# Loading the experts' weights in 2 MB parts through a ring of six buffers

## The chip, the core and the metric

The kernel runs on one core of one Trainium2 chip. The metric is the time of one execution on the device in microseconds; the median of several runs counts. All arithmetic on the path that matters here is in float32.

## What is computed

The reference is a model of two blocks over 512 tokens of width 1024. The first block and the first half of the second are mixers (attention, recurrences, projections). The change lies in the last stage, a mixture of experts: each token goes to 4 of 32 experts, each with a weight `w1` of 1024 x 2048 and a weight `w2` of 1024 x 1024. Cut to that:

```python
logits = ht @ router_w + router_b
top_val, top_idx = lax.top_k(logits, TOP_K)          # 4 of 32
gates = jax.nn.softmax(top_val, axis=-1)
...
def expert_block(args):
    idx, e = args
    u = clamped_swiglu(h_pad[idx] @ w1[e] + b1[e])
    return u @ w2[e] + b2[e]
...
y = jnp.zeros((t + 1, d)).at[slot_tok].add(y_slots * slot_gate[:, None])
```

After it a residual sum and a layer norm give the output of 512 x 1024.

## The kernel before

Engines are named as in the profile: PE is TensorE, PEld its weight loads, DVE VectorE, ACT ScalarE, POOL GpSimd, SP SyncE, whose queue issues most DMAs.

**The experts' stage** (`experts`, from L2173 on) goes through the 32 experts in an order that is worked out on the chip: place 0 is expert 0, the others are ordered by how many tokens they have. Each place has a fixed number of blocks of 32 rows (`BLOCKS`): one place has 4, sixteen have 3, fifteen have 2, mixed as the list `PLACES` (L35) says; 82 blocks in all. The index of an expert is read into a register of SP (L2200 and after), and its loads are addressed by it.

For place j the program issues `up` of j (L2300 on; first matrix product, 8 parts of the weight `w1`), then `down` of the place before it (L2360 on; second product, 4 parts of `w2`), so that the activation of j runs on DVE and ACT beside `down` of j - 1. Only place 0 is done alone: `up`, transposes, `down`. Inside `up` at fixed parts stand the other PE jobs: finding the rows of later experts (`slots`, at part 0), the transposes of the activations of the place before (`turn_u`, at part 2), and the transposes of the next place's rows (`turned`, at part 4), after which the gather for the place after that is issued on POOL. `down` ends with one scaling on DVE and one accumulating scatter on POOL for each block (L2380, L2381).

**A part** is 1 MB: 128 partitions of 2,048 float32, 8,192 bytes. An expert has 8 parts of `w1` (one for each 128 rows of the input) and 4 of `w2` (two 128-row pieces side by side), 12 MB; 32 experts make 384 parts. A block of a part takes 8 matmuls of 512 columns in `up` and 16 of 256 columns in `down`, as the profile counts them.

**The ring.** `ring` (L1829) sets the size of a part and makes a pool with 12 buffers, `EARLY`, on its first call, and a pool with one more on its second, when the experts' stage begins and space has come free; `RING` is 13. `load` (L1838) takes the buffers in turn: load n goes to buffer n modulo 13, and its DMA, issued on SP (L1843), waits until PE's last read of that buffer. So when a part has been used, the load that stands 13 later can be issued. The loads stand in SP's queue in the order in which PE uses them. In the tile framework the DMAs of SP use eight completion semaphores in turn, so that a load also waits for the landing of the DMA eight before it.

**The first twelve loads** are issued by `mix_out` (L1860), before the experts' stage, as `self.pre`: 8 parts of `up` and 4 of `down` of expert 0. They run beside the end of the mixer: the normalised rows are stored to `hd` in four stores of 512 KB from POOL (L1940), and the gather of the first expert's rows (L2274) reads `hd`. In `experts` a further line (L2184) would load what is missing of the first twelve; with `EARLY` 12 its range is empty. `up` and `down` take a part from `self.pre` while there are any, and call `load` afterwards.

**The end.** After the last `down` a check for experts with more rows than their places hold is made; for these inputs its branch is not taken. `final` (L2421 on) reads the scattered sums into the first four ring buffers, adds, normalises and stores the output.

Of the kernel before, what the change touches and what calls it, by code (L numbers as in the profile page):

```python
# [17 lines left out]
P = 128  # L18
# [3 lines left out]
D = 1024  # L22
KD = D // P
# [4 lines left out]
E = 32  # L28
TOPK = 4
LIMIT = 7.0  # L30
RING = 13
EARLY = 12


PLACES = [0, 17, 18]  # L35
# [1764 lines left out]
class Tail:  # L1800
# [20 lines left out]
    def weight(self, e):  # L1821

        w1, w2 = (self.k.I[n] for n in ("exp_w1", "exp_w2"))
        if isinstance(e, int):
            return (lambda i: w1[e, i * P:(i + 1) * P]), (lambda i: w2[e, i])
        return ((lambda i: w1[bass.ds(e, 1), i * P:(i + 1) * P].rearrange("a p n -> p (a n)")),
                (lambda i: w2[bass.ds(e, 1), i].rearrange("a p h n -> p (a h) n")))

    def ring(self, ctx):  # L1829

        k = self.k
        k.usize = 2 * D
        if not hasattr(self, "rings"):
            self.rings = [k.pool("rawx", 1, None, ctx, "left")] * EARLY
        else:
            self.rings += [k.pool("rawy", 1, None, ctx, "left")] * (RING - EARLY)

    def load(self, part):  # L1838

        self.loads += 1  # L1840
        n = self.loads % RING
        w = self.k.t(self.rings[n], [P, self.k.usize], tag=f"raw{n}", bufs=1)
        self.k.nc.sync.dma_start(w if len(part.shape) == 2 else w.rearrange("p (h n) -> p h n", h=2), part)  # L1843
        return w

    def mix_out(self, b):

        k = self.k
        nc, tc = k.nc, k.tc
        x3 = self.x3 = [k.t(b.mixp, [P, D], tag=f"ar{t}") for t in range(NT)]  # L1850
        self.yd = b.yd
        with ExitStack() as st:
            pw = k.pool("mow", 2, None, st)
            self.psp = b.psp
            for t in range(NT):
                nc.sync.dma_start(x3[t], b.base[t * P:(t + 1) * P])

            one, two = self.weight(0)
            self.loads = -1
            self.pre = [self.load(part) for part in ([one(i) for i in range(KD)] + [two(i) for i in range(4)])[:EARLY]]  # L1860
            self.first = k.t(b.po, [P, P], tag="po")

            def finish(t, nh, ps, r):
                ns = slice(nh * S, (nh + 1) * S)
                x = x3[t][:, ns]
                if nh == 0:
                    r.stats = k.t(pw, [P, 2, 6], tag="bn")
                    r.xT = k.t(pw, [P, KD, P], tag="xT")
                nc.vector.tensor_add(x, x, ps)
                pt = k.t(b.pa, [P, S], tag="pa")  # L1870
                for j in range(4):
                    nc.tensor.transpose(pt[:, j * P:(j + 1) * P], x[:, j * P:(j + 1) * P], k.ident)
                nc.scalar.copy(r.xT[:, nh * 4:nh * 4 + 4], pt.rearrange("p (a n) -> p a n", a=4))
                nc.vector.bn_stats(r.stats[:, nh], x)
                if nh:
                    self.norm(t, r, pw)


            n = 2 * NT
            rs = [SimpleNamespace() for _ in range(NT)]  # L1880
            routes = []
            done = []
            for i in range(n + 4):
                if i < 2:
                    done.append(b.made[i])
                elif i < n:
                    ps = k.t(b.pb, [P, S], tag="pb")
                    done.append((ps, b.product(*divmod(i, 2), ps)))
                with tc.issue_after(done[-1][1]):
                    if 1 <= i <= n:  # L1890
                        t, nh = divmod(i - 1, 2)
                        finish(t, nh, done[i - 1][0], rs[t])
                        if nh:
                            routes.append(self.route(t, rs[t], pw))
                    if i >= n:
                        routes.reverse()
                    routes = [g for g in routes if next(g, routes) is not routes]
            self.after = self.slots(pw, [0], self.first)
# [276 lines left out]
    def experts(self, ctx):  # L2175
        k = self.k
        nc, I, tc = k.nc, k.I, k.tc
        self.prev = None
        self.mw = mw = k.pool("moew", 2, None, ctx, "right")
        xg = [k.t(mw, [P, D], tag="xg") for _ in range(2)]  # L2180
        for x in xg:
            nc.vector.memset(x, 0.0)
        xg = self.gather(self.idx[:, 0:1])
        self.pre += [self.load(self.weight(0)[1](i)) for i in range(EARLY - KD, 4)]  # L2184
        self.biases(ctx)
        x = self.turned(xg)
        self.places_of(self.late)
        self.slots(mw, [1])
        xg = self.gather(self.idx[:, 1:2])

        self.gt2 = k.t(self.late, [P, 256], tag="gt2q")
        for n in range(4):
            v = MR["gt2"]
            nc.gpsimd.dma_start(self.gt2[n * 32:(n + 1) * 32], k.modr[v:v + 1, n * 256:(n + 1) * 256].to_broadcast([32, 256]))
        before = None
        for j in range(E):
            if j == 0:
                e, takes = 0, k.ident[:, 0:1]
            else:
                e = nc.values_load(self.order[0:1, j:j + 1], engines=[mybir.EngineType.SP], min_val=0, max_val=E - 1)  # L2200
                takes = self.takes[:, j:j + 1]
            nxt = SimpleNamespace(nb=BLOCKS[j], rows=self.rows[:, j], gate=self.gate[:, j])
            one, nxt.two = self.weight(e)
            then = {}
            if j % 2 == 0 and j + 2 < E:
                then[0] = lambda: self.slots(mw, [j + 2, j + 3])
            if before is not None and before.uT is None:
                then[2] = lambda: self.turn_u(before)
            if j + 1 < E:
                def following():  # L2210
                    nonlocal x, xg
                    x = self.turned(xg)
                    if j + 2 < E:
                        xg = self.gather(self.idx[:, j + 2:j + 3])
                if j:
                    then[4] = following
            self.up(nxt, x, takes, one, then)
            if before is not None:
                self.down(before)
            if j == 0:  # L2220
                self.turn_u(nxt)
                self.down(nxt)
                following()
                nxt = None
            before = nxt
            with tc.issue_after(self.sc):
                if j in (2, 10):
                    self.last_rows(j // 8)
                if j == E - 1:
                    self.final_rows()  # L2230
            if j in LB:
                with tc.issue_after(self.sc):
                    self.last_bias(*divmod(LB.index(j), NT))
        self.turn_u(before)
        self.down(before)

        self.rest(self.late)
        most = nc.values_load(self.over[0:1, E:E + 1], min_val=0, max_val=S)
        with tc.If(most > 0):
            self.make_lists(mw)  # L2240
            with tc.For_i(0, E, 1) as e:
                n = nc.values_load(self.over[0:1, bass.ds(e, 1)], min_val=0, max_val=S)
                with tc.If(n > 0):
                    self.more(e, 0)
                    for blk in range(1, NT):
                        with tc.If(n > P * blk):
                            self.more(e, blk)
# [49 lines left out]
    def up(self, st, x, takes, units, then):  # L2297


        k = self.k  # L2300
# [4 lines left out]
        with ExitStack() as order:  # L2305
# [3 lines left out]
            for i in range(KD):  # L2309
                if i in then:  # L2310
                    then[i]()
                w = self.pre.pop(0) if self.pre else self.load(units(i))
                for b in range(st.nb):
                    for c in range(4):
                        last = mm(ps[b][c * 32:(c + 1) * 32], x[:, i, b * 32:(b + 1) * 32], w[:, c * S:(c + 1) * S],  # L2315
# [43 lines left out]
    def down(self, st):  # L2359

        k = self.k
# [3 lines left out]
        of = lambda b: ps[b // 2][:, b % 2 * 256:(b % 2 + 1) * 256]  # L2365
        with tc.issue_after(self.prev):
            for c in range(4):
                w = (self.pre.pop(0) if self.pre else self.load(st.two(c))).rearrange("p (h n) -> p h n", h=2)
                for h in range(2):
                    for b in range(st.nb):  # L2370
                        for n in range(4):
# [107 lines left out]
def host(inp):  # L2479

    f = lambda a: np.ascontiguousarray(np.asarray(a))
# [8 lines left out]
    g = lambda n: np.asarray(inp[n])[0]  # L2490
# [19 lines left out]
    for n, a in (("ml_g", g("ml_norm_g")), ("gla_g", g("gla_norm_g")), ("final_g", inp["final_g"]),  # L2510
# [14 lines left out]
           "w_in_2": f(g("w_in_2")), "ada_w": f(g("ada_w_2")), "rwkv_w2": f(g("rwkv_w2_2")), "rwkv_a2": f(g("rwkv_a2_2")),  # L2525
           "rwkv_g2": f(g("rwkv_g2_2")), "w_uq": f(wuq), "w_kv": np.stack([g("w_uk_2"), g("w_uv_2")]),
           "pos": f(np.asarray(inp["positions_2"])[0].reshape(NT, P).T), "w_o": f(g("w_o_2")),
           "router_w": f(g("router_w_2")), "exp_w1": f(g("exp_w1_2")), "exp_w2": f(g("exp_w2_2").reshape(E, 4, 2, P, D).transpose(0, 1, 3, 2, 4)), "b1": f(g("exp_b1_2")),
           "b2": f(g("exp_b2_2"))}
    out.update(constants())  # L2530
    return out
# [15 lines left out]
```

## Time and profile before

| what | value |
|---|---|
| median of 3 runs | 1888.42 us (1884.67 to 1901.79) |
| the profiled execution, its own time | 1900.38 us |
| its span, first to last instruction | 1898.6 us |
| mean granted TensorE clock | 0.966 |
| PE busy | 1796.5 us, 95% of the span |
| experts' loads | 384 of 1,024 KB |

The profile shows one execution. The slices divide the span in forty, about 47.5 us each, and give the busy share in tenths; DMA is the mean busy share of the core's 16 DMA engines. A wait names the instruction that waited, what released it, the sum of the waiting times, how often, and the longest. PE's busy time counts pipelined matmuls, so 99% need not mean that it worked at its peak.

### The profile page before, as it was taken

What the parts mean: (1) busy time and instruction counts of PE and PEld (TensorE: products, weight loads), DVE (VectorE), ACT (ScalarE), POOL (GpSimd) and SP (SyncE); (2) the same over time, 40 slices, a digit from 0 to 9 for tenths busy, and PEclk for the clock granted to TensorE, in tenths of its full rate; (3) what the DMA queues carried; (4) which work ended last, traced back from release to release, by engine and by line L of the source; (5) the groups of instructions that cost most, each with busy time, mean ns of one, the idle gap of its engine ahead of it and who ended that gap; (6) DMA issues with size and microseconds to landing.
All of it is one profiled execution on the core that took longest, in us unless ns stands there. A gap on an engine that the chain in (4) does not pass through costs nothing. (4 is left out here: it accounts for less than half of the span.)

```text
span 1898.6 us, 40110 instructions
## 1 busy us (share of the span) xinstructions
PE 1796.5 (95%) x16798; PEld 1105.9 (58%) x16799; DVE 832.3 (44%) x2057; ACT 472.5 (25%) x1050; POOL 313.4 (17%) x285
## 2 busy tenths in 40 slices
PE   8999999998899999979999999999999999999982
PEld 8887788786798977744343434443444444344431
DVE  6756744756865577633233323232323222232323
ACT  4434323453345533311111111111111111111101
POOL 1010001032100014111113221123120212021102
PEclk9998979999899999989999999999999999999996
DMA  8255441655210013669999999999999999999994
GB/s 278 83 192 178 126 125 40 200 166 159 49 43 19 23 56 112 250 251 354 409 412 397 406 403 415 400 412 404 412 403 410 396 413 400 405 404 408 408 398 150
DMA packets 145212, 520.69 MB, mean 274 GB/s; under 512 B 29392, under 2 KB 71936, under 8 KB 95712
## 3 DMA queue, kind: packets, MB, share of 16 engines
q1 hardware_dynamic: 121360, 487.91, 65.8%
q0 software_dynamic: 18000, 22.06, 4.8%
q10 hardware_dynamic: 5664, 8.09, 1.4%
q8 instruction: 133, 2.18, 0.5%
q14 instruction: 55, 0.45, 0.1%
HBM read 504.30 MB, written 24.43 MB: 278 GB/s over the span
## 5 line engine op out<-in xcount | busy, mean ns | idle before, releaser
L2315 PE MATMUL h<-raw,x 128*32 128x512 f32 x5248 | 620.4, 596 | 4.5 <-DMA raw<-in_exp_w 4.4
L2315 PEld LDWEIGHTS h<-raw,x 128*32 128x32 f32 x5248 | 171.0, 110 | 346.8 <-issue 313.6
L2372 PE MATMUL y<-raw,uT 128*32 128x256 f32 x5248 | 293.2, 381 | 7.3 <-DMA raw<-in_exp_w 4.4
L2372 PEld LDWEIGHTS y<-raw,uT 128*32 128x32 f32 x5248 | 180.3, 110 | 126.8 <-issue 20.9
L2381 POOL DMA_INDIRECT yd<-y,rows x82 | 131.2, 1601 | 727.1 <-DVE y L2380 711.8
L2333 DVE TENSOR_TENSOR h<-h,bias 128x512 f32<-128x512 f32 x82 | 56.3, 687 | 309.9 <-PE h L2315 309.9
L2291 DVE TENSOR_SCALAR x<-ps,modc 128x128 f32<-128x128 f32 x128 | 52.0, 410 | 181.9 <-ACT x L2294 178.5
L2380 DVE SCALAR_TENSOR_TENSOR y<-y,gate,gt2q 128x256 f32<-128x256 f32 x82 | 35.2, 479 | 174.5 <-PE y L2372 174.5
L2341 ACT ACTIVATE sth<-sg 128x256 f32<-128x256 f32 x82 | 34.2, 417 | 266.5 <-DVE sg L2339 266.5
L155 PE MATMUL mm<-hh,hi 128*128 128x512 f32 (+1 forms) x248 | 97.7, 394 | 0.0
L156 PE MATMUL mm<-lo,hh 128*128 128x384 f32 (+4 forms) x288 | 95.4, 331 | 2.0 <-DVE lo L150 2.0
L156 PE MATMUL mm<-hl,hi 128*128 128x512 f32 (+1 forms) x248 | 96.4, 389 | 0.0
L155 PE MATMUL mm<-hi,hh 128*128 128x384 f32 (+4 forms) x288 | 95.8, 334 | 0.0
L157 PE MATMUL mm<-hh,lo 128*128 128x512 f32 (+1 forms) x248 | 95.0, 383 | 0.0
L157 PE MATMUL mm<-hi,hl 128*128 128x384 f32 (+4 forms) x288 | 94.4, 330 | 0.0
L150 DVE TENSOR_TENSOR lo<-raw,hi 128x1024 fp32r<-128x1024 f32 (+5 forms) x77 | 76.5, 997 | 40.0 <-ACT hi L149 38.9
L149 ACT CAST hi<-raw 128x1024 fp32r<-128x1024 f32 (+5 forms) x77 | 66.4, 863 | 101.8 <-PE mm L156 47.6
L2294 ACT ACTIVATE x<-ps,modc 128x128 f32<-128x128 f32 x128 | 57.1, 457 | 122.8 <-PE ps L2287 112.2
L2357 ACT COPY uT<-ps 128x512 f32<-128x512 f32 (+1 forms) x49 | 24.2, 518 | 161.4 <-PE ps L2354 157.9
L966 DVE SCALAR_TENSOR_TENSOR acc<-mraw,cact,acc 128x1024 f32<-128x1024 f32 x42 | 53.8, 1280 | 20.6 <-DMA mraw<-in_ada_w 20.4
L155 PEld LDWEIGHTS mm<-hi,hh 128*128 128x128 f32 x288 | 57.4, 199 | 7.3 <-issue 5.1
L2322 ACT COPY bias<-ps 128x512 f32<-128x512 f32 x32 | 18.8, 586 | 169.1 <-PE ps L2320 169.1
(720 smaller groups left out, 2730.4 us busy)
## 6 DMA issues: line engine op xcount, KB each, us to landing
raw<-in_exp_w SPq DMA_DIRECT2D x384, 1024.0 KB
mraw<-in_ada_w SPq DMA_DIRECT2D x48, 512.0 KB
raw<-in_w_in SPq DMA_DIRECT2D x30, 512.0 KB
raw<-in_w_in SPq DMA_DIRECT2D x16, 384.0 KB
raw<-in_w_out SPq DMA_DIRECT2D x8, 512.0 KB
raw<-in_w_o SPq DMA_DIRECT2D x16, 256.0 KB
yd<-x SPq DMA_DIRECT2D x5, 512.0 KB
x<-in_x SPq DMA_DIRECT2D x4, 512.0 KB
```

The source lines that it names most:

```text
L149: nc.scalar.copy(hi, r)
L150: nc.vector.tensor_sub(lo, r, hi)
L155: mm(out, ah, bh, start=first, stop=False)
L156: mm(out, ah, bl, start=False, stop=False)
L157: return mm(out, al, bh, start=False, stop=last)
L966: nc.vector.scalar_tensor_tensor(out=self.acc, in0=raw, scalar=self.act[:, kk:kk + 1], in1=self.acc, op0=OP.mult, op1=OP.add)
L2291: k.nc.vector.tensor_scalar(out=x[:, kk], in0=ps[:, j * P:(j + 1) * P], scalar1=col(2, kk), scalar2=col(3, kk), op0=OP.mult, op1=OP.add)
L2294: k.nc.scalar.activation(x[:, kk], ps[:, j * P:(j + 1) * P], AF.Identity, scale=col(2, kk), bias=col(3, kk))
L2315: last = mm(ps[b][c * 32:(c + 1) * 32], x[:, i, b * 32:(b + 1) * 32], w[:, c * S:(c + 1) * S], start=i == 0, stop=i == KD - 1)
L2333: nc.vector.tensor_add(h, ps, bias)
L2372: last = mm(of(b)[n * 32:(n + 1) * 32], st.uT[b][:, h, c * 32:(c + 1) * 32], w[:, h, n * 256:(n + 1) * 256], start=c + h == 0 and b % 2 == ...
L2381: s = nc.gpsimd.indirect_dma_start(out=yd, out_offset=bass.IndirectOffsetOnAxis(ap=st.rows[:, b:b + 1], axis=0), in_=y, in_offset=None, bo ...
```

## The change

A part becomes 2 MB: 128 partitions of 4,096 float32, 16,384 bytes. `w1` has 4 such parts for each expert, `w2` has 2. The host lays the weights out so that each part's 16,384 bytes of a partition stand together. The ring has six buffers, all of which exist from the first call; the first six loads (12 MB) are issued where the first twelve were. `up` and `down` load a buffer at every second of their steps and read a half of it in each, so matmuls and their order are as before. The buffer comes free after the second half.

```diff
-RING = 13
-EARLY = 12
+RING = 6
+EARLY = 6
...
         if isinstance(e, int):
-            return (lambda i: w1[e, i * P:(i + 1) * P]), (lambda i: w2[e, i])
-        return ((lambda i: w1[bass.ds(e, 1), i * P:(i + 1) * P].rearrange("a p n -> p (a n)")),
-                (lambda i: w2[bass.ds(e, 1), i].rearrange("a p h n -> p (a h) n")))
+            return (lambda i: w1[e, i]), (lambda i: w2[e, i])
+        return tuple((lambda i, w=w: w[bass.ds(e, 1), i].rearrange("a p n -> p (a n)")) for w in (w1, w2))
 
     def ring(self, ctx):
 
         k = self.k
-        k.usize = 2 * D
+        k.usize = 4 * D
         if not hasattr(self, "rings"):
             self.rings = [k.pool("rawx", 1, None, ctx, "left")] * EARLY
-        else:
-            self.rings += [k.pool("rawy", 1, None, ctx, "left")] * (RING - EARLY)
 
     def load(self, part):
...
-        self.k.nc.sync.dma_start(w if len(part.shape) == 2 else w.rearrange("p (h n) -> p h n", h=2), part)
+        self.k.nc.sync.dma_start(w, part)
...
-            self.pre = [self.load(part) for part in ([one(i) for i in range(KD)] + [two(i) for i in range(4)])[:EARLY]]
+            self.pre = [self.load(part) for part in [one(i) for i in range(4)] + [two(i) for i in range(2)]]
...
-        self.pre += [self.load(self.weight(0)[1](i)) for i in range(EARLY - KD, 4)]
...
-                w = self.pre.pop(0) if self.pre else self.load(units(i))
+                if i % 2 == 0:
+                    unit = self.pre.pop(0) if self.pre else self.load(units(i // 2))
+                w = unit[:, i % 2 * 2 * D:(i % 2 + 1) * 2 * D]
...
-                w = (self.pre.pop(0) if self.pre else self.load(st.two(c))).rearrange("p (h n) -> p h n", h=2)
+                if c % 2 == 0:
+                    unit = self.pre.pop(0) if self.pre else self.load(st.two(c // 2))
+                w = unit[:, c % 2 * 2 * D:(c % 2 + 1) * 2 * D].rearrange("p (h n) -> p h n", h=2)
```

In `host` the arrays are reshaped to match: `exp_w1` to 32 x 4 x 128 x 4096 and `exp_w2` to 32 x 2 x 128 x 4096.

## Rows read from the trace of the kernel before

**Rows 1.** The page: PE and DMA in the forty slices, and the experts' loads.
```profile
...
PE   8999999998899999979999999999999999999982
...
DMA  8255441655210013669999999999999999999994
GB/s 278 83 192 178 126 125 40 200 166 159 49 43 19 23 56 112 250 251 354 409 412 397 406 403 415 400 412 404 412 403 410 396 413 400 405 404 408 408 398 150
...
raw<-in_exp_w SPq DMA_DIRECT2D x384, 1024.0 KB
```

**Rows 2.** Two windows: length, busy us by engine (instructions), PE clock, DMA share, GB/s.
```profile
868.00:1814.00 946.00, 938.77 (x11056) 408.99 (x11052) 262.69 (x680) 128.29 (x288) 189.07 (x137) 1.00 1.02 405
1814.00:1866.50 52.50, 41.35 (x542) 16.72 (x534) 10.12 (x29) 3.43 (x7) 7.44 (x6) 1.00 0.85 334
```

**Rows 3.** PE's longest wait, 868 to 1814 us: total us, times, longest.
```profile
PE ps L2069 <- DVE f L2057: 5.8, 7, 1.6
```

**Rows 4.** PE's longest waits, 1814 to 1867 us.
```profile
PE y L2372 <- DMA raw<-in_exp_w: 4.4, 5, 2.0
PE h L2315 <- DMA raw<-in_exp_w: 4.4, 6, 1.1
```

**Rows 5.** The waits of SP's queue, 880 to 1200 us.
```profile
SPq L1843 <- PE h L2315: 172.1, 76, 5.6
SPq L1843 <- PE y L2372: 48.6, 35, 2.9
```

**Rows 6.** The waits of SP's queue, 1205 to 1845 us.
```profile
SPq L1843 <- DMA raw<-in_exp_w: 480.5, 233, 3.3
```

**Rows 7.** DMA view, 947 to 957 us: packets; a queue's packets, MB, share.
```profile
DMA packets 577, 4.21 MB, mean 421 GB/s; under 512 B 65, under 2 KB 65, under 8 KB 65
...
q1 hardware_dynamic: 575, 4.18, 100.6%
```

**Rows 8.** DMA view, 1886 to 1896 us (the stores of the output).
```profile
DMA packets 452, 1.65 MB, mean 165 GB/s; under 512 B 48, under 2 KB 48, under 8 KB 452
...
q1 hardware_dynamic: 452, 1.65, 40.7%
```

**Rows 9.** DMA view, 444 to 450 us.
```profile
DMA packets 1169, 2.25 MB, mean 375 GB/s; under 512 B 74, under 2 KB 80, under 8 KB 1168
...
q1 hardware_dynamic: 1168, 2.23, 99.9%
```

**Rows 10.** DMA view, 33 to 40 us (q10: 128 rows of 12,288 bytes).
```profile
q10 hardware_dynamic: 144, 1.57, 59.3%
q1 hardware_dynamic: 688, 1.07, 41.3%
```

**Rows 11.** DMA view, 778 to 1077 us.
```profile
q1 hardware_dynamic: 14274, 102.50, 84.4%
...
raw<-in_exp_w SPq DMA_DIRECT2D x98, 1024.0 KB
```

**Rows 12.** DMA view, 778 to 868.5 us.
```profile
raw<-in_exp_w SPq DMA_DIRECT2D x22, 1024.0 KB
```

**Rows 13.** Timeline of PE, 1857 to 1867 us: start, us, what, idle before.
```profile
1861.60 1.93 PE L2372 MATMUL y<-raw,uT 128*32 128x256 f32 x32 [0.71 <-SPq L2239]
1864.52 1.93 PE L2372 MATMUL y<-raw,uT 128*32 128x256 f32 x32 [0.99 <-SPq L2239]
```

**Rows 14.** Timeline of POOL, 795 to 828 us.
```profile
812.78 0.58 POOL L1940 DMA_DIRECT2D hd<-ar  x1 [1.76 <-ACT pos L1975]
821.53 1.11 POOL L2274 DMA_INDIRECT xg<-hd,idx  x1 [8.17 <-DMA hd<-ar]
```

**Rows 15.** Line L1940, the four stores of `hd`.
```profile
DMA to landing us min/median/max: 7.9/8.3/8.7
```

**Rows 16.** Timeline, 815 to 840 us.
```profile
825.78 1.97 PE L2287 MATMUL ps<-ident,xg 128*128 128x128 f32 x8 [7.52 <-DMA xg<-hd,idx]
```

More of the change, by code (lines that the diff above doesn't have):

```diff
@@ L2527, in host @@
            "pos": f(np.asarray(inp["positions_2"])[0].reshape(NT, P).T), "w_o": f(g("w_o_2")),
-           "router_w": f(g("router_w_2")), "exp_w1": f(g("exp_w1_2")), "exp_w2": f(g("exp_w2_2").reshape(E, 4, 2, P, D).transpose(0, 1, 3, 2, 4)), "b1": f(g("exp_b1_2")),
+           "router_w": f(g("router_w_2")), "exp_w1": f(g("exp_w1_2").reshape(E, 4, 2, P, 2 * D).transpose(0, 1, 3, 2, 4).reshape(E, 4, P, 4 * D)),
+           "exp_w2": f(g("exp_w2_2").reshape(E, 2, 4, P, D).transpose(0, 1, 3, 2, 4).reshape(E, 2, P, 4 * D)), "b1": f(g("exp_b1_2")),
            "b2": f(g("exp_b2_2"))}
```

## The prediction

> **What bounds the kernel now.** I read the page's forty slices first, then single windows, then who waited for whom on TensorE (PE) and on SyncE's DMA issues (SP), and at the end the DMA view, cut into stretches in which one kind of transfer ran alone.
>
> The slices show two programs in one [rows 1]. Up to about slice 18 the DMA is partly idle. From slice 19 on PE reads 9 and DMA reads 9 in every slice up to the last ones, at some 400 GB/s: this is the experts' stage, in which 384 loads of 1,024 KB come in. Two engines at 9 don't say which one sets the end. The two windows do [rows 2]: from 868 to 1814 us PE is busy 938.8 of 946.0 us and the DMA share is 1.02; from 1814 to 1866.5 us PE is busy 41.35 of 52.5 us. The waits agree: before 1814 us PE waits for no weights at all, its longest sum is 5.8 us on a DVE tile [rows 3]; after it, it waits for `raw<-in_exp_w` at part after part [rows 4]. So PE and DMA run side by side for 946 us, each full, and the weights come in last: PE finishes when the last part has landed and its 32 matmuls (1.93 us) are done [rows 13]. What sets the end of the stage is the DMA engines' work from 868 us, where they idled last, to 1864 us. PE has 52.5 - 41.35 = 11.15 us to give at the end, no more.
>
> What gates the issue of a load changes on the way: between 880 and 1200 us SP waits for PE to free a buffer (172.1 + 48.6 us) [rows 5], from 1205 us on for an older load (480.5 us, 233 times) [rows 6]. In the first part the ring is the gate; it costs nothing now, as enough loads are in flight while SP waits.
>
> **The change, part by part.** The sum is made on the profiled execution: span 1898.6 us, its own time 1900.38 us, 12 us over the median of the runs, 1888.42 us.
>
> *Packets.* A load was 128 rows of 8,192 bytes, eight on each DMA engine; it becomes 128 rows of 16,384. The bytes stay; the number of packets halves, and so does the number of completion writes. No 16 KB load to SBUF stands in the trace, so I compare sizes. In 947 to 957 us only weights moved: 575 packets, 65 of them under 512 bytes, took 100.6% of 16 engines for 10 us, that is 160.96 us over 510 packets, 315.6 ns each [rows 7]. The output's stores have 4 KB rows: 40.7% of 160 us over 452 - 48 = 404 packets, 161.2 ns [rows 8]. Loads with 2 KB rows: 99.9% of 96 us over 1,168 - 80 = 1,088, 88.1 ns [rows 9]. Twice 161.2 is 6.8 ns more than 315.6; four times 88.1 is 36.8 ns more, 12.3 for each of three packets. So a packet has a fixed part of 6.8 to 12.3 ns. Of 2 MB each engine saves eight of them and one completion write, nine times 6.8 to 12.3, 61 to 111 ns; I take 80. At 868.5 us 22 loads had been issued [rows 12], so 362 parts, 181 pairs, lie in the stretch that counts: 11 to 20 us less, I take **-14.5 us** (181 x 0.080).
> The bound on the other side is the only load with larger rows, 12 KB: 59.3% of 16 engines for 7 us over 128 packets, 519 ns, where 1.5 x 315.6 is 473 [rows 10]. Another queue used 41.3% at the same time, so I take it as shared service and not as the price of a large packet; it stays as the bad end.
>
> *The ring, 13 x 1 MB to 6 x 2 MB.* A buffer comes free when its second part has been used. At 868.5 us nine parts had been used (22 - 13); then six buffers and four refilled pairs make 20 parts issued instead of 22, and at the end of the first expert (12 parts used) 24 instead of 25. From there the DMA is always full, so what is missing stays missing: 1 MB is 2.5 us (4.18 MB in 10 us) [rows 7], 2 MB would be 5. I take **+2.5 us**.
> Whether the DMA then runs dry: at 1077 us, the thinnest place I found, 98 loads (102.76 MB) had been issued and 102.50 MB moved, in which 0.5 to 2.1 MB of other loads are counted [rows 11]. So 0.8 to 2.4 MB were in flight, 1.9 to 5.7 us. The change takes 2.5 us of that and issues one part's work later (1.9 us with two blocks [rows 13], twice that with four); 0 to 6 us of idle DMA in all, one for one at the end. I take 0, as the higher reading covers 2.5 + 1.9, and price the rest as a rival.
>
> *The end.* The last buffer holds two parts, so PE still has two to do when it lands, not one: **+1.9 us** [rows 13].
>
> *The start.* The first 12 MB are loaded beside four 512 KB stores of `hd`; the last store is issued at 812.78 us, and the gather of the first expert's rows follows its landing at 821.53 us [rows 14]. The stores take 7.9 to 8.7 us to land beside the loads [rows 15]; the gather of the same 512 KB with hardly a load in flight needs 4.25 us until PE starts on it [rows 14, 16]. The loads cost it some 4 us; with packets twice as long it may be 0 to 4 us more. I take **+2 us**; the whole stage moves by it.
> The Trainium skill bears on this (DMA: Bandwidth & Descriptors, "Queues, rings and completion order"): each DMA engine goes round its queues and changes only at a packet's end. By that rule a store of eight rows an engine waits eight times 315 ns longer, 2.5 us, and the sum would be -7.6 us; the stores' 8 us beside loads agree with it.
>
> *Nothing for the rest.* Half of SP's issues go, but SP idles in its waits for most of the stage [rows 5, 6]. Its wait for the load eight before goes too, since no more than six are ever open; PE's release gates all through, and with six buffers open the DMA has up to 12 MB queued where eight loads gave 8. The view of a half buffer that PE reads costs no instruction. The load that stood in `experts` covered an empty range (EARLY - KD is 4), so its removal changes nothing. The host's new order of weights is outside the time. The scatters and gathers get slower as the stores do, but each is waited for an expert later, some 30 us; if that cover failed, a wait of theirs would fall on PE, which has 11 us to give.
>
> **Sum:** -14.5 + 2.5 + 1.9 + 2 = -8.1 us. 1900.38 becomes 1892.3, a ratio of 0.9957; on the median of 1888.42 us that is **1880.4 us**. A measurement of this kernel can tell about 1%, 18.9 us, from no change, so I forecast no change that can be told.
>
> **Rivals.**
> *PE's own end.* If a packet's fixed part is at the high end (-20), the DMA no longer ends last. PE's slack is 11.15 us and the start's 2 us come on top: at most -9 to -11, **1878 us**. For it: PE is at 99% up to 1814 us [rows 2]. Either way no gain over 11 us is there to be had; that is why faster by over 1% has little chance.
> *No gain by size* (or 16,384-byte rows cut in two again, so that the change doesn't do what it says). Then only the costs are left, 2.5 + 1.9 + 2 = +6.4 us, **1894.8 us**. For it: the fixed part is read from other stretches, with stores and other loads; against: both comparisons give the same sign.
> *The ring runs dry.* If the smaller ring lets the DMA idle 4 to 6 us in all between 1030 and 1110 us, of the -8.1 about -3 is left, **1885 us**. For it: SP waits up to 5.6 us for PE there [rows 5].
> *Large packets are dear* (the other side). If a 16 KB row costs 519/473 of its bytes' price as the 12 KB rows did, 9.7% on the 362 parts of 2.48 us (898 us) is +87 us, and with the other costs +94: 1982 us. It decides from little on: 1.4% dearer per byte (12.5 us) with the 6.4 us makes 1% of the time. At 3%, say, it gives 33 us, **1922 us**. Against: from 2 to 8 KB the price per byte only falls, and the 12 KB row is shared.
>
> **How the numbers follow.** Forecast 0.50, PE's end 0.12, no gain 0.17, dry ring 0.09, dear packets 0.12. The first four lie within 1% by their sums, 0.88; the three runs shown spread over 17 us, for which I move 0.08 of the first two to faster and leave 0.01 of the others to slower. So faster 0.08, same 0.79, slower 0.13. The likeliest case alone reaches from 1877 us (the gain capped by PE's 11 us) to 1888 us (-11 with the costs at their upper ends, 5 + 1.9 + 4). The range takes in the case without gain, and the spread of the runs below: 1867 to 1898 us; dear packets are left out.
>
> **What would show it.** Right: 192 loads of 2,048 KB; half the packets of 8 KB and over on the weights' queue; the mean rate of a stretch with weights alone up from 421 to about 430 GB/s; PE waiting for weights later than 1814 us, and for under 8 us; two parts of matmuls behind the last landing; PE's first expert about 2 us later. Wrong: a rate at or under 421 GB/s (no gain, or dear packets; PE's first wait for weights then comes long before 1814 us), a DMA share under 1.0 between 880 and 1200 us (dry ring), or PE waiting for nothing but itself up to its end (PE's own end).

## The result, and the profile after

The changed kernel took 1912.6 us in the median of its runs, the kernel before, run beside it on the same chip, 1900.7 us. The ratio is **1.0089, with a 95% interval of 1.0066 to 1.0112**: slower by 0.9%, some 17 us, where 8 us less had been forecast. Three of the changed kernel's twenty runs, at 2669 to 5792 us, were disturbed and are left out of the ratio; the median of the other seventeen is 1910.9 us. The medians thus lie only 10 to 12 us apart; the stage's own time, below, bears out the 17 us of the ratio.

The whole executions are not the best scale. The first matmul of `up` came at 827.7 us in the profiled execution before and at 817.4 us after, because the mixer ahead of it took 10 us less that time. So I measure the experts' stage by itself, from the start of the first `up` matmul to the end of the last `down`: **1038.8 us before, 1056.3 us after, 17.5 us more.**

The page of the changed kernel, the same lines as in [rows 1], and its two large groups of matmuls (L2313 is `up`, L2372 is `down`):

```profile
PE   8999999999899999789999999999999999999993
...
DMA  7266531564110031859999999999999999999995
GB/s 269 83 196 187 153 99 54 193 194 132 38 47 19 12 117 51 353 200 372 414 408 400 382 404 411 409 413 394 356 396 391 407 397 403 381 408 402 380 413 186
...
L2313 PE MATMUL h<-raw,x 128*32 128x512 f32 x5248 | 630.6, 605 | 0.1
...
L2372 PE MATMUL y<-raw,uT 128*32 128x256 f32 x5248 | 293.0, 382 | 0.7 <-ACT uT L2355 0.7
...
raw<-in_exp_w SPq DMA_DIRECT2D x192, 2048.0 KB, 12.0
```

The loads are as announced, 192 of 2,048 KB. But the slices of the stage no longer stay near 400 GB/s: 356, 382, 380 stand among them. And PE waits 0.1 and 0.7 us before its matmuls, so it no longer waits for weights. The windows say more (length, busy us of PE, PEld, DVE, ACT and POOL with instructions, PE's clock, DMA share, GB/s); the first two answer to [rows 2], the third is the whole stage, the others are one place where the stage loses time:

```profile
868.00:1814.00 946.00, 922.70 (x10758) 407.49 (x10754) 257.84 (x668) 123.43 (x279) 180.80 (x133) 0.98 1.01 398
1814.00:1866.50 52.50, 48.89 (x562) 20.91 (x558) 11.96 (x34) 6.39 (x13) 7.77 (x5) 0.97 1.01 412
...
817.40:1873.70 1056.30, 1026.29 (x11971) 457.68 (x11970) 286.05 (x754) 136.69 (x308) 196.62 (x145) 0.98 0.98 388
...
1076.00:1085.00 9.00, 7.93 (x110) 4.78 (x102) 4.74 (x11) 0.42 (x1) 2.95 (x3) 1.00 0.99 418
1085.00:1088.00 3.00, 0.69 (x36) 0.63 (x40) 2.27 (x5) 0.00 (x0) 2.92 (x3) 0.60 1.05 417
1088.00:1092.00 4.00, 4.00 (x21) 0.79 (x16) 0.21 (x1) 0.17 (x1) 2.53 (x3) 0.50 1.00 349
1093.00:1098.00 5.00, 4.54 (x40) 2.17 (x38) 1.64 (x4) 2.65 (x6) 1.03 (x1) 1.00 0.81 256
```

From 868 to 1814 us PE was busy for 938.8 us before and for 922.7 after: it got less done in the part in which it used to have no gap. Its longest waits there answer to [rows 3], and SP's from 1205 to 1845 us to [rows 6] (sum, times, longest):

```profile
PE ps L2066 <- DVE f L2054: 7.2, 6, 2.6
PE ps L1991 <- DVE pick L1988: 6.3, 8, 0.8
PE ps L2318 <- DVE x L2287: 4.5, 3, 1.5
PE ps L2283 <- ACT uT L2355: 4.4, 10, 0.5
...
SPq L1840 <- PE h L2313: 321.7, 62, 12.1
SPq L1840 <- PE y L2372: 157.0, 40, 4.6
```

PE now waits 22.4 us for DVE and ACT; before it was 5.8 us for `f` [rows 3] and 1.2 us for ACT's `uT`, 7 in all. And SP, which waited for older loads, now waits for PE to free a buffer, up to 12.1 us at once. Where PE is late, the next load is late: in the last window above, behind PE's gap, the DMA falls to 256 GB/s.

The jobs that wait are the small ones of `slots`: the two groups of `pick` (L1991), which find the rows of two later experts, and the row spread (L2066), which needs DVE's `f`, made from both. PE's timeline of the changed kernel at one place (start, us, what, matmuls, idle before):

```profile
1080.84 1.05 PE L1991 MATMUL ps<-val,pick 128*128 128x3 f32 x8
1082.68 1.05 PE L1991 MATMUL ps<-val,pick 128*128 128x3 f32 x8 [0.78 <-DVE pick L1988]
1083.66 1.05 PE L2313 MATMUL h<-raw,x 128*32 128x512 f32 x2
1087.31 0.61 PE L2066 MATMUL ps<-f,ident 128*32 128x4 f32 x32 [2.59 <-DVE f L2054]
1087.75 5.93 PE L2313 MATMUL h<-raw,x 128*32 128x512 f32 x30
```

The pick groups stand side by side, and only one group of `up` (2 matmuls in the profile) stands between them and the spread. Before, one group of `up` stood between the picks and seven more ahead of the spread. **So the order of PE's queue has changed, though the diff moves no matmul.** The orders of the two programs, as built, at the places that prepare slots (P pick, U0 and U1 parts 0 and 1 of `up`, S spread, T and X transposes, D `down`; the number behind x counts the program's matmuls; the profile shows two for each of them, and one for a transpose):

```
before  ... D3 x16  P.14 x4  U0 x1  P.15 x4  U0 x7  S.14 x16  T x4  U1 x8  T x2  X0 x4 ...
after   ... D3 x16  P.14 x4  P.15 x4  U0 x1  S.14 x16  U0 x7  U1 x8  T x6  X0 x4  X1 x4 ...
```

In eight of thirteen such places from place 4 on the picks are side by side after the change, in none before. The tile framework writes each engine's queue when the kernel is built, by a time that it models for every instruction, the landing of a load among them; with other loads it chose another order.

The second loss is the clock. In the windows above PE's clock is 1.00 (2.4 GHz) up to 1085 us and 0.50 (1.2 GHz) from 1088 to 1092; the 30 matmuls of `up` there take 5.93 us, where 16 at full clock take 1.92 us. Read in windows of 1 us, PE ran at 1.2 GHz for 3.4 us between 868 and 1814 us before, and for 40.9 us, in nine spells, after. The same 11,971 matmuls of the stage kept PE busy for 1017.4 us before and 1026.3 us after, +8.9; its idle time grew from 21.4 to 30.0 us, +8.6. **By this account half of the 17.5 us is clock, half is waiting.** But the second half is a balance of two sums: over the stage PE's waits for DVE and ACT grew from 10.1 to 28.9 us, and its waits for weights, 8.8 us before [rows 4], are gone. The first of the new waits only took the place of the old ones; e5 and e9 below tell the two losses apart.

### The profile page after: what moved, and what is told of

Read it like the earlier page. It is cut to its first block, busy times and chain, and to the rows that moved or that the text cites. A ratio compares the mean times of both kernels' runs of the same rounds, so it can differ in the third digit from the quotient of the medians.

```text
span 1906.5 us, 39357 instructions
## 1 busy us (share of the span) xinstructions
PE 1793.7 (94%) x16798; PEld 1107.7 (58%) x16799; DVE 835.5 (44%) x2057; ACT 472.4 (25%) x1050; POOL 312.0 (16%) x285
## 5 line engine op out<-in xcount | busy, mean ns | idle before, releaser
L2313 PE MATMUL h<-raw,x 128*32 128x512 f32 x5248 | 630.6, 605 | 0.1
L2313 PEld LDWEIGHTS h<-raw,x 128*32 128x32 f32 x5248 | 178.8, 111 | 359.6 <-issue 353.8
L2372 PE MATMUL y<-raw,uT 128*32 128x256 f32 x5248 | 293.0, 382 | 0.7 <-ACT uT L2355 0.7
L2372 PEld LDWEIGHTS y<-raw,uT 128*32 128x32 f32 x5248 | 185.1, 111 | 114.4 <-issue 20.7
```

Source lines behind the costliest of these rows:

```text
L2372: last = mm(of(b)[n * 32:(n + 1) * 32], st.uT[b][:, h, c * 32:(c + 1) * 32], w[:, h, n * 256:(n + 1) * 256], start=c + h == 0 and b % 2 == ...
```

## The experiments

In all of them PE's queue is fixed by edges that only order it and add no wait, one from each matmul to the next:

```diff
+        pe = [i for i in k.nc.cur_bb.bb.instructions[start:] if i.engine == mybir.EngineType.PE]
+        seq = [pe[s + j] for s, n in ORDER for j in range(n)]
+        for p, q in zip(seq, seq[1:]):
+            tc.add_manual_dep(q, p.name, mybir.DependencyInfo(mybir.DependencyClass.NoSync, mybir.DependencyReason.DATA),
+                              reason="order of TensorE's queue")
```

`ORDER` lists the stage's 6,202 matmuls of the program in the wanted order, as runs of a first number and a count; the method with these lines is `pin`. In this table "stage" is as above, "idle" is the stage less PE's busy time in it, "1.2 GHz" the time at that clock from 868 to 1814 us, "up" the mean of one matmul of `up`. These four are read from one profiled execution of each kernel; the ratios rest on 6 to 17 runs of the kernel named and on those of the kernel before beside it:

| kernel | loads | order | stage us | PE idle us | 1.2 GHz us | up ns | ratio to before (95%) |
|---|---|---|---|---|---|---|---|
| before | 1 MB | its own | 1038.8 | 21.4 | 3.4 | 596 | |
| after | 2 MB | its own | 1056.3 | 30.0 | 40.9 | 605 | 1.0089 (1.0066 to 1.0112) |
| e1 | 2 MB | of before | 1035.0 | 19.6 | 3.4 | 596 | 0.9979 (0.9949 to 1.0008) |
| e2 | 1 MB | of after | 1054.8 | 30.7 | 37.6 | 604 | 1.0091 (1.0057 to 1.0126) |
| e3 | 1 MB, ring of 12 | of before | 1041.3 | 22.7 | 3.4 | 597 | 1.0026 (1.0000 to 1.0052) |
| e4 | 2 MB in two DMAs | of before | 1045.3 | 24.3 | 6.8 | 597 | 1.0022 (0.9995 to 1.0048) |
| e5 | 2 MB | slots of before | 1036.2 | 23.3 | 0 | 595 | 1.0002 (0.9976 to 1.0028) |
| e6 | 2 MB | a third | 1033.3 | 15.2 | 0 | 595 | 0.9984 (0.9953 to 1.0015) |
| e7 | 1 MB | a third | 1040.6 | 17.3 | 2.8 | 597 | 0.9996 (0.9963 to 1.0029) |
| e9 | 2 MB | of after, spreads of before | 1046.1 | 24.0 | 34.0 | 605 | 1.0031 (0.9995 to 1.0067) |
| e10 | 2 MB | of after, one part moved | 1056.4 | 34.0 | 27.2 | 603 | 1.0084 (1.0042 to 1.0127) |

**Order or loads? e1 and e2.** e1 is the changed kernel with PE's queue in the order of before, 341 runs:

```diff
+ORDER = [
+    (0, 8), (70, 5), (8, 1), (75, 8), (9, 9), (83, 4), (18, 8), (87, 8), (26, 4), (95, 8), (30, 20), (103, 4),
...
+        self.pin(start)
         self.rest(self.late)
```

> The changed kernel with TensorE's queue in the experts' stage held to the order that it had before the change (the other engines' orders then fall into place). Theory, the order: the 2 MB loads cost nothing, and what made the change slower is that the instructions of TensorE were laid out in another order, in which it waits for VectorE and ScalarE. Then the stage from the first matmul of the experts to the last is no longer 17.5 us longer than before but shorter: 1038.8 us before, about 1030 us here, as my prediction had it (-8 us, ratio 0.996); TensorE waits for weights only at the end. Rival, the loads: larger loads or the shorter ring are the cause whatever the order; then the ratio stays near 1.009 and the stage near 1056 us.

e2 is the kernel before, its loads untouched, with the same two lines and the order of the changed one, 275 runs.

> The kernel before, 13 buffers of 1 MB, with TensorE's queue held to the order of the changed kernel. Theory, the order: the stage takes what it takes in the changed kernel, 1056 us instead of 1038.8, TensorE waits for a DVE or ACT tile about 22 us in all, never for weights, and the ratio is about 1.009. Rival, the loads: no change, ratio 1.000, stage 1039 us.

The timeline of PE in e1 at the place shown above:

```profile
1090.76 1.05 PE L2030 MATMUL ps<-val,pick 128*128 128x3 f32 x8
1091.74 1.04 PE L2365 MATMUL h<-raw,x 128*32 128x512 f32 x2
1092.72 1.05 PE L2030 MATMUL ps<-val,pick 128*128 128x3 f32 x8
1093.70 1.92 PE L2365 MATMUL h<-raw,x 128*32 128x512 f32 x14
1097.22 0.43 PE L2105 MATMUL ps<-f,ident 128*32 128x4 f32 x32 [1.61 <-DVE f L2093]
```

Windows of e1: the whole stage, the same stretch as in [rows 2], and the place itself:

```profile
828.70:1863.70 1035.00, 1015.41 (x11971) 445.14 (x11970) 285.91 (x754) 137.08 (x308) 198.36 (x145) 1.00 0.99 397
...
868.00:1814.00 946.00, 936.75 (x11051) 407.75 (x11046) 262.69 (x680) 128.32 (x288) 188.84 (x137) 1.00 1.01 405
...
1095.00:1098.00 3.00, 1.39 (x42) 0.76 (x36) 2.40 (x5) 0.00 (x0) 2.92 (x3) 1.00 1.04 410
1098.00:1102.00 4.00, 3.97 (x37) 1.66 (x39) 0.41 (x1) 1.96 (x6) 2.58 (x4) 1.00 1.02 397
```

And of e2, the whole stage, with its longest waits from 868 to 1814 us:

```profile
825.10:1879.90 1054.80, 1024.15 (x11971) 455.46 (x11970) 286.59 (x754) 136.73 (x308) 196.41 (x145) 0.98 0.99 389
```

```profile
PE ps L2102 <- DVE f L2090: 8.6, 8, 2.6
PE ps L2027 <- DVE pick L2024: 6.3, 8, 0.8
PE ps L2366 <- DVE x L2337: 4.5, 3, 1.5
PE ps L2333 <- ACT uT L2403: 4.3, 10, 0.5
```

The old order takes the whole loss away, and the new order brings it into the kernel before with its 1 MB loads: the same waits, almost sum by sum, seven spells of 1.2 GHz (37.6 us) where the changed kernel has nine (40.9 us), +16.0 us in the stage. The order is the cause, shown from both sides. No run holds a kernel to its own order; that e2 comes within 1.5 us of the changed kernel speaks against a price of the edges themselves. The stage of e1 had been expected at about 1030 us and took 5 more. The loads themselves are worth 1035.0 - 1038.8 = -3.8 us, e1's ratio says -4.0 us, with an interval that takes in no change.

**Which of the moved jobs? e5.** Only those edges of e1 stay that touch a pick or a spread:

```diff
         for p, q in zip(seq, seq[1:]):
+            if p not in SLOTS and q not in SLOTS:
+                continue
```

> The changed kernel, with only the matmuls of slots (the places of later experts' rows, L1991 and L2066 in the changed kernel's numbering) held to where they stood in TensorE's queue before, fourteen times in the stage; transposes and biases stay where the change put them. Theory, the slots: they carry the loss, since in the changed order their two groups stand next to each other and TensorE waits for VectorE between and behind them. Then the stage is 1035 to 1040 us and the ratio 0.998 to 1.002. Rival, the whole order: the transposes of the next rows, back to back in the changed order, cost as much; then half of the 21 us stays, stage 1046 us, ratio 1.004.

Its windows (868 to 1814 us, then the stage) and its longest waits in the first:

```profile
868.00:1814.00 946.00, 928.67 (x10984) 412.96 (x10976) 262.93 (x680) 127.91 (x288) 188.90 (x137) 1.00 1.01 406
...
825.10:1861.30 1036.20, 1012.91 (x11971) 454.09 (x11970) 286.02 (x754) 136.68 (x308) 198.41 (x145) 1.00 0.99 396
```

```profile
PE ps L2109 <- DVE f L2097: 6.4, 4, 1.6
PE ps L2377 <- DVE x L2346: 6.0, 4, 1.5
PE ps L2342 <- ACT uT L2414: 4.1, 10, 0.5
```

20.1 of e1's 21.3 us come back by the slots alone. What the table shows besides: e5 still waits 16.5 us for DVE and ACT, 9.5 more than before, and is as quick as before. Its clock never falls, and PE's waits for weights are gone as in the changed kernel: these 9.5 us took the place of the wait at the end. PE's idle time alone is not what the change cost. Against e5, the changed kernel's 20.1 us are 13.4 us more of PE busy with the same matmuls (1026.29 less 1012.91) and 6.7 us more of idle time.

**What does the clock fall behind? e9 and e10.** Two more runs split the two moves at the slots. e9 holds the spreads only, so that the picks stay side by side:

```diff
 SLOTS = {i for s, n in (
-    (26, 44), (356, 24), (732, 24), (1146, 24), (1526, 24), (1904, 24), (2282, 24), (2662, 24), (3042, 24),
...
+    (30, 16), (54, 16), (364, 16), (740, 16), (1154, 16), (1534, 16), (1912, 16), (2290, 16), (2670, 16), (3050, 16),
...
```

> The changed kernel, its 2 MB loads untouched; on TensorE's queue only the row spreads of the slots (32 matmuls of 4 columns as the profile counts them, which wait for DVE's f) are held at the places they had in the kernel before, eight or nine groups of up behind the second pick. The two pick groups stay together, as in the changed kernel, with TensorE's wait of 0.8 us between them. Read: the granted clock. In the changed kernel TensorE ran at 1.2 GHz in nine spells between 868 and 1814 us, 41 us in all; in the kernel before in one spell of 3.4 us. Theory 'picks together' (the two pick groups side by side, 3 columns each, are what TensorE's clock falls behind): at least six spells stay, TensorE's clock in 868 to 1814 us reads 0.98 or 0.99, one up matmul takes 601 ns or more in the mean, only some 6 us of waits for f go, and the experts' stage takes 1046 to 1052 us. Theory 'late rows' (the clock falls behind the wait of up to 2.6 us for f): at most two spells stay, the clock reads 1.00, an up matmul 595 to 597 ns, the stage 1036 to 1041 us.

e10 keeps the order of after, but moves one group of `up` between the picks in the eight places:

```
-D3 x16  P.14 x4  P.15 x4  U0 x1  S.14 x16  U0 x7
+D3 x16  P.14 x4  U0 x1  P.15 x4  S.14 x16  U0 x7
```

> The changed kernel with its own order on TensorE's queue but for eight places: where the two pick groups of the slots stood side by side, the one group of up that stood behind the second is put between them, so that the row spreads follow the second pick at once. TensorE's idle time hardly changes by that (the wait of 0.8 us for the second pick goes, the wait for f grows from up to 2.6 to some 3.5 us). Theory 'picks together': at most two spells at 1.2 GHz are left between 868 and 1814 us, an up matmul takes 595 to 598 ns, TensorE's waits stay at 20 us or more, and the stage takes 1037 to 1044 us, so that about half of the loss is the clock. Theory 'late rows': the spells stay (six or more, clock 0.98), an up matmul 602 ns or more, the stage 1052 to 1058 us.

PE's timeline of e9, and a window of it that begins behind the picks:

```profile
1087.41 1.05 PE L2034 MATMUL ps<-val,pick 128*128 128x3 f32 x8
1089.24 1.05 PE L2034 MATMUL ps<-val,pick 128*128 128x3 f32 x8 [0.78 <-DVE pick L2031]
```

```profile
1091.00:1097.00 6.00, 4.97 (x60) 1.15 (x52) 3.06 (x5) 0.17 (x1) 5.70 (x5) 0.53 1.00 393
```

The same two views of e10:

```profile
1087.11 1.05 PE L2024 MATMUL ps<-val,pick 128*128 128x3 f32 x8
1091.62 0.61 PE L2099 MATMUL ps<-f,ident 128*32 128x4 f32 x32 [3.45 <-DVE f L2087]
```

```profile
1088.00:1096.00 8.00, 4.55 (x58) 1.52 (x60) 3.59 (x6) 0.17 (x1) 6.75 (x5) 0.57 1.01 390
```

Each run came out as one theory had it, and each against the other: in e9 the clock falls seven times (34.0 us) with picks side by side and a single wait for `f`, of 1.0 us; in e10 seven times (27.2 us) with the picks apart and eight waits for `f`, of 0.8 to 3.5 us. So neither theory holds alone. Either move is enough to bring seven spells, where the kernels with the slots in their old places (before, e1, e3, e4, e5) have none to two.

For a single fall no wait is needed, though. The spell of the kernel before begins behind the second of its picks (1025.69 us), while PE works on `up` without a gap; and two of the nine of the changed kernel (from 1420 and 1618 us) come where four matmuls of `up` stand between the picks and PE waits for nothing:

```profile
1026.68 3.34 PE L2315 MATMUL h<-raw,x 128*32 128x512 f32 x14
...
1027.00:1028.00 1.00, 1.00 (x8) 0.20 (x3) 1.00 (x2) 0.00 (x0) 1.00 (x2) 0.51 0.96 401
...
1420.00:1421.00 1.00, 1.00 (x10) 0.22 (x5) 0.87 (x5) 0.00 (x0) 0.69 (x2) 0.56 0.92 393
```

The first two lines are of the kernel before, the last of the changed one. What the spells share is the place: in all eleven profiles each one that begins between 868 and 1814 us does so 0.3 to 6.2 us after the start of a second pick group. At which of these places the clock falls differs even with the order held (1027 us before, 1543 us in e1). Whether it is the few columns of the small jobs or the waits around them that lower it, no run separates.

Put side by side with e5, e9 also gives the price of the clock by itself: PE's waits for DVE and ACT are the same (16.4 and 16.5 us from 868 to 1814 us), the clock is not (34.0 us at 1.2 GHz and none), and the stage takes 9.9 us more.
The Trainium skill (TensorE: Matmul & The Clock Gate, "HAM oscillation — how this bites in real kernels") tells of the same pattern with waits for loads: each wait lets the clock fall, and the next group of matmuls begins at the low one. These traces agree in part: groups behind waits of 0.8 to 3.5 us for DVE run at 1.2 GHz, but the spells in the rows above came with no wait ahead of them.

**The terms of the sum. e3 and e4.** e3 is the kernel before with twelve buffers, 1 MB less:

```diff
-RING = 13
+RING = 12
```

> The kernel before with a ring of 12 buffers of 1 MB (the 13th left out), TensorE's queue in the order of before. Both theories of the order: +2.5 us at the end (1 MB less on the way when the DMA fills up for good), ratio 1.001, stage 1041 us; if the ring runs dry, 4 to 8 us, ratio up to 1.004. If the shorter ring is the cause of the loss: near 1.009.

e4 is e1, but each 2 MB buffer is filled by two loads with rows of 8,192 bytes:

```diff
-        self.k.nc.sync.dma_start(w, part)
+        for h in range(2):
+            self.k.nc.sync.dma_start(w[:, h * 2 * D:(h + 1) * 2 * D], part[:, h * 2 * D:(h + 1) * 2 * D])
```

> The changed kernel in the order of before, with each 2 MB buffer filled by two loads of 1 MB, whose rows are 8,192 bytes: the new ring without the new packets. Beside the first run it shows what packets of 16,384 bytes are worth: by my prediction 14.5 us less for the DMA engines, of which TensorE leaves 11; so here the stage is 1045 us, +6 against before, ratio 1.003, against 1030 us in the first run. If packet size is worth nothing, both take the same.

e3: +2.5 us in the stage, +4.9 us by its ratio. e4: +6.5 us in the stage, +4.2 us by its ratio. From e4 to e1 only the rows' length and the count of loads change: 1045.3 - 1035.0 = 10.3 us less (by the ratios 0.0043 x 1895.6, the median of before beside them, 8.2 us; by the means of their twelve runs each 7.6 us, with an interval of about 3 to 12).

**A better order. e6 and e7.** A build with the modelled landing time of a load set to nothing writes a third order, in 115 runs: at most of the places that prepare slots it has five of the program's matmuls between the picks and eight ahead of the spread. e6 holds the changed kernel to it, e7 the kernel before; from e1 to e6 the edit is `ORDER` alone:

```diff
-    (364, 16), (396, 4), (405, 119), (556, 4), (592, 8), (524, 32), (560, 32), (600, 136), (756, 5), (736, 4),
...
+    (364, 16), (396, 4), (405, 331), (756, 5), (736, 4), (761, 8), (740, 16), (769, 7), (780, 1), (776, 4),
...
```

> The 2 MB loads with a third order of TensorE's queue: the one that the scheduler writes when it takes the loads as landing at once. In it the other jobs stand where the program has them, with one or two parts of matmuls between a job and the one that needs its result. If waits for VectorE and ScalarE are what the order costs, TensorE has fewer of them than before (7 us) and reaches the end of the weights earlier; the DMA engines then set the end and the stage is 1031 to 1035 us, ratio 0.993 to 0.998. If this order waits more, it shows in TensorE's waits and the stage is longer than the 1035 us of the first run.

> The kernel before (13 x 1 MB) with the same third order. The DMA engines set its end already, so a better order is worth nothing here: stage 1037 to 1040 us, ratio 1.000, only with more waiting for weights at the end. Beside the run before it, it shows what the 2 MB loads are worth with the best order: 4 to 8 us.

The longest waits of e6 from 868 to 1814 us, and its window:

```profile
PE y L2400 <- DMA raw<-in_exp_w: 2.9, 4, 1.3
PE h L2341 <- DMA raw<-in_exp_w: 1.2, 1, 1.2
```

```profile
868.00:1814.00 946.00, 941.50 (x11056) 394.85 (x11058) 259.32 (x691) 129.65 (x290) 189.89 (x138) 1.00 1.02 409
```

PE waits for nothing but weights, the clock never falls, and 409 GB/s come in where 405 did. The stage takes 5.5 us less than before, the best of all; the ratio of 0.9984 does not tell it from no change. In e7 the same order is worth nothing, as expected: 1.8 us more than before, with 12.0 us of waiting for weights over the stage against 8.8. From e7 to e6 the larger loads are worth 7.3 us in the stage, within the 4 to 8 expected, and 2 us by the ratios, which don't tell it from nothing.

## Why the prediction was wrong

**The step that failed** stands under "Nothing for the rest": the view of a half buffer that PE reads "costs no instruction". That is so: the matmuls are the same 11,971. But from it I took that PE's side stays as it was, and the sections ahead of the prediction say "matmuls and their order are as before". The diff fixes no order; it is made anew at each build. That cost 21.3 us (after less e1), more than all terms of the sum together, and it fell on the engine that I had at 99% [rows 2], with 11 us to give at the end. All rivals let PE keep its work and moved the weights; none let PE itself become slower. "PE's own end" had the right engine, but as a cap on a gain; its sign, PE waiting for no weights up to its end, did come. Not all of the distance from 1880.4 to 1912.6 us is the change: the forecast stood on a median of 1888.4 us, and the kernel before took 1900.7 beside the changed one, 12 of the 32 us.

**The packets** were priced right in kind and a little high: -14.5 us, with 11 to 20 as ends; e4 to e1 gave -10.3 in the stage, or -12.0 without the second part that e1 has behind its last landing and e4 has not. The DMA view of the changed kernel from 940 to 950 us, with weights alone, answers to [rows 7]:

```profile
DMA packets 293, 4.27 MB, mean 427 GB/s; under 512 B 32, under 2 KB 32, under 8 KB 32
...
q1 hardware_dynamic: 291, 4.24, 100.7%
```

161.1 us over 291 - 32 = 259 packets is 622 ns, where two of the old ones took 631: 9 ns less, within the 6.8 to 12.3 that were read from smaller rows. The rate rose from 421 to 427 GB/s; 430 was forecast. "Large packets dear" and "no gain by size" are refuted.

**The ring and the end** were forecast at +2.5 and +1.9, 4.4 us. The end was right: behind the last landing e1 has 64 matmuls of `down`, 3.66 us, where before 32 took 1.93 [rows 13], +1.7 us:

```profile
1860.06 3.66 PE L2424 MATMUL y<-raw,uT 128*32 128x256 f32 x64 [1.35 <-SPq L2276]
```

The ring looks priced too low: e3 gave +2.5 for 1 MB less of it, but e4, the ring of pairs with one part behind the last landing, +6.5, that is 4 us more (by its ratio under 2, with an interval that takes in no change). What makes up the difference is not shown. The dry ring did not show by itself: in e1 the DMA share is 1.01 from 868 to 1814 us and PE waits for no weights there. Together, -12.0 + 6.5 + 1.7 is the -3.8 us of e1, where these terms were forecast at -10.1.

**The start** was forecast at +2 us for longer packets beside the last store of `hd`. POOL's gather waited 8.17 us for it before [rows 14]; in e1 and, with 8 KB rows, in e4:

```profile
822.57 1.10 POOL L2322 DMA_INDIRECT xg<-hd,idx x1 [9.60 <-DMA hd<-ar]
```

```profile
815.45 1.10 POOL L2323 DMA_INDIRECT xg<-hd,idx x1 [9.37 <-DMA hd<-ar]
```

That is +1.4 and +1.2 us, and by this pair alone only 0.2 us would be the packet's length. But the wait scatters by 2 us between kernels with the same rows: over all profiles it is 7.56 to 9.51 us in the five with 8 KB rows (before, e2, e3, e4, e7), 8.6 in the mean, and 9.53 to 10.68 us in the six with 16 KB rows (after, e1, e5, e6, e9, e10), 10.0 in the mean. So longer rows go with +1.4 us, near the forecast in size and in reason. The rule of the Trainium skill that I drew on (DMA: Bandwidth & Descriptors, "Queues, rings and completion order") gave an estimate of 2.5 us; these profiles scatter too much to decide between the two, and the 8 us of the stores, which I took as agreement, don't test it.

With the order held, then, the sum would have been -3.8 us in the stage and +1.4 ahead of it, about -2 us against a forecast of -8.1: no change that can be told, as forecast, for reasons that were mostly right. What was timed was the order.

## What to carry to other kernels

Where a build step writes the engines' queues, a change in one transfer's size can rewrite the queue of an engine that the diff never touches. Compare the order of instructions on each engine of both kernels before calling a part of a change free, and hold the order by edges to see what the change itself is worth. On a TensorE that runs without gaps, keep large matmuls between small jobs that wait for each other: here the moved jobs were paid as waits and, from e5 to e9 with the same waits, again as clock. Waits that fit into a slack elsewhere, as in e5, cost nothing.

## What the runs showed of the hardware that was not expected

A wait of 1.61 us for `f` behind 14 matmuls of `up` left PE at 2.4 GHz (e1, 1095 to 1102 us: 1.00). Two pick groups of 3 columns with a wait of 0.78 us between them and 2 matmuls of `up` behind were followed by 1.2 GHz within the next wait, of 2.59 us, and not only at its end (after, 1085 to 1088 us: 0.60). The 30 matmuls behind, most of them at that clock, took 5.93 us, where 1.92 us for 16 make 3.6. The clock also fell behind picks while PE had work all the time (before, 1027 us: 0.51). e9 against e5 puts the price of 34 us at the low clock at some 10 us of stage, from one profile each.
